# Modulation sums in pairs, table work ordered behind a weight product, one scan for both directions, first norms' squares on TensorE

## The chip, the cores and the metric

The kernel runs on one core of a Trainium2 chip. The metric is the device time of one execution in microseconds. Three timed runs of the kernel before took 3287.81, 3289.54 and 3294.22 us; the median is 3289.54. One further execution was taken with the hardware profiler, and all durations below are from that one.

## What is computed

One layer of a diffusion backbone on 256 latent tokens (`x`) and 256 context tokens (`ctx`), width 2048, everything in float32. Cut to the parts that the change touches:

```python
mod   = silu(c) @ w_ada + b_ada          # 18432 columns: shift, scale, gate of 3 sublayers
mod_c = silu(c_ctx) @ w_ada + b_ada      # the same weights for the context

def ffn(x, m, gain, wg, wu, wd):         # sublayers 1 and 3
    h = rmsnorm(x, gain) * (1 + m.scale) + m.shift
    return x + 0.5 * m.gate * ((silu(h @ wg) * (h @ wu)) @ wd)

x, ctx = ffn(x, mod[0], ...), ffn(ctx, mod_c[0], ...)
proj   = modulated_norm(x, mod[1]) @ w_in           # [S5 | hyena v,x1,x2 | gate_A | gate_B]
proj_c = modulated_norm(ctx, mod_c[1]) @ w_in[:, :1024]
for direction in (forward, reverse):                # 64 groups x 64 complex states
    last  = scan(proj_c)                            # s[t] = Abar * s[t-1] + Bbar u[t]
    y    += Re(C @ scan(proj[S5], start=last))
mixed = (sigmoid(gate_A) * glu(y) + sigmoid(gate_B) * hyena(proj)) @ w_out
x = x + mod[1].gate * mixed
x = ffn(x, mod[2], ...)
return rmsnorm(x, final_g)
```

Each weight is read once per execution.

## The kernel before

**Products.** A float32 weight piece is loaded, cast on ACT to a high part (`wh`, L177, 128x2048) and its rest is made by two DVE subtractions (`wl`, L181, 128x1024 each). Activations are split likewise. `mm3` (L184 to L187) adds three 128x512 matmuls of the type fp32r into one PSUM bank: high by high, high by low, low by high; `mmc` (L194, L196) does it with the activations' two parts side by side.

**Order.** The order in which each engine runs its instructions is fixed when the program is built: a scheduler runs a timeline of its own and places each instruction when that timeline says its inputs are there. `tc.issue_after(ins)`, which the change uses, adds one more condition: the instruction stands behind `ins` on its engine.

**Stages** (us of the profiled execution). From 0 to about 136: the first modulation columns on PE (`ada_pe`, L218 to L238, bank `adacc`, then transposes by a selection matrix, `adsum` L233), the S5 constants, the hyena filters (`kps`, `aps`, `sps`, `hps`), and the first norms (`rstd_of`): 16 squares on ACT per stream, added on DVE (latent, `xl`) and POOL (context, `xc`) at L315. From 136 to 1745: the first FFN, 22 column blocks of 6 weight pieces (gate `pg`, up `pu`, down `pd`), 132 steps of 48 matmuls. At each step `background()` advances two generators: two steps of `ada_rest`, one of `s5_tables`.

`ada_rest` makes the other modulation columns: DVE multiplies raw columns of `w_ada` by the vector and sums them into an accumulator `ac` (L253, L255, 128x512); a matmul with a 128x32 matrix of ones adds the 128 partitions into 32 rows of a bank (L260), ACT copies the 32 rows (L261), and four transposes close a group of four. `ada_vec` does 6 groups of two column blocks with two vectors each (`ns` is 2: latent and context) and 4 groups of four blocks with one (`ns` is 1): 40 sums in all.

`s5_tables` makes, for 8 blocks q and 2 directions d, products on POOL (`win`, cmul at L597 and L600), their transposes on PE (`wtp`, L889, two sets of four), products on POOL (`gt`, L901 and L904) and kernel taps on PE (`kp`, L914, two sets of eight 32-column matmuls in four row groups). `adacc`, its transposes, `wtp` and `kp` all use the one bank of the pool `pc`.

From 1745 on: the up and S5 projections, context carries (a tree of complex products, DVE for direction 0 and POOL for direction 1, L1067 to L1075), then the latent scan, about 1963 to 2034: 31 steps of five `tensor_tensor`, direction 0 on DVE and direction 1 on POOL (L1085 to L1089), with the read-out `yb` (L1111) behind it. PE's work beside it is the output gates, 16 calls of `project` (one is 96 matmuls of 128x256, with the same casts and subtractions for its weights). Then the hyena branch, the merge, the second FFN, to 3283.

Of the kernel before, what the change touches and what calls it, by code (L numbers as in the profile page):

```python
# [19 lines left out]
P = 128  # L20
# [108 lines left out]
def _body(tc, nc, I, out, dbg, es):  # L129
# [53 lines left out]

    def mm3(ps, H, L, xH, xL, first, last):  # L184
# [53 lines left out]
    def ada_vec(nts, ap_):  # L238


        ns = 2 if nts[0] < 20 else 1
        sb = ap_.tile([P, 512], F32, name="adsb", tag="adsb", bufs=1)
        per = 4 // ns
        for i, nt in enumerate(nts):
            acc = [ap_.tile([P, 512], F32, name=f"ac{s}", tag=f"ac{s}", bufs=1) for s in range(ns)]
            for q in range(8):
                raw = ap_.tile([P, 2, 512], F32, name="raw2", tag="raw2", bufs=2)
                sync.dma_start(raw, w_ada[q * 256:(q + 1) * 256, nt * 512:(nt + 1) * 512].rearrange("(k p) n -> p k n", p=P))
                for g in range(2):
                    k = q * 2 + g  # L250
                    for s in range(ns):
                        if k == 0:
                            dve.tensor_scalar(acc[s], raw[:, g], S32[:, k, s:s + 1], None, op0=ALU.mult)  # L253
                        else:
                            dve.scalar_tensor_tensor(acc[s], raw[:, g], S32[:, k, s:s + 1], acc[s], op0=ALU.mult, op1=ALU.add)  # L255
# [47 lines left out]
    def rstd_of(tp, streams, sq, pl, tg):  # L303
# [3 lines left out]
        ns = len(streams)  # L307
        for k in range(KD):
            for xs, r, eng in streams:
                if k == 0:  # L310
# [45 lines left out]
    def prescale(T, sub, xs, s):  # L356


        for i in range(4):
            sh = modT[:, sub * 3 * KD + 4 * i:sub * 3 * KD + 4 * i + 4, s:s + 1].to_broadcast([P, 4, 2])  # L360
            act.copy(T[i][:, :, 516:518], sh)
            dve.tensor_tensor(T[i][:, :, 0:2], sh, T[i][:, :, 516:518].bitcast(F32), ALU.subtract)
            dve.tensor_copy(T[i][:, :, 258:260], zero.unsqueeze(2).to_broadcast([P, 4, 2]))
        for k, t in enumerate(pieces(T)):
            g = gsc[sub][:, k, s:s + 1]
            h, l = both(t)[:, 1], both(t)[:, 0]
            act.activation(h, xs[k], AF.Identity, scale=g)
            dve.scalar_tensor_tensor(l, xs[k], g, h.bitcast(F32), op0=ALU.mult, op1=ALU.subtract)
# [415 lines left out]
    def ada_first():  # L784
# [4 lines left out]
        rstd_of(py, ((xl, r1[0], dve),), ("sq", 2), pb, "b")  # L789
# [4 lines left out]
        rstd_of(py, ((xc, r1[1], pool),), ("sq", 2), pb, "b")  # L794
# [59 lines left out]
    def s5_tables(tp):  # L854

        kv = kD.rearrange("(b r) q (g n) -> r b (q g) n", b=4, g=2)
        for q in range(8):
# [14 lines left out]
            for d in range(2):  # L872
# [33 lines left out]
                yield  # L906
                for g2 in range(2):
                    kp = pc.tile([P, P], F32, name="kp", tag="c")
                    hs = slice(64 * g2, 64 * g2 + 64)
                    for ri in range(2):  # L910
                        for b4 in range(4):
                            e0 = d
                            bo = ((d * 2 + ri) * 4 + b4) * 16
                            pe.matmul(kp[32 * b4:32 * b4 + 32, :], bc_[hs, bo:bo + 32],  # L914
                                      gt[hs, b4, ri, e0:e0 + 8, :].rearrange("p e h -> p (e h)"), start=(ri == 0), stop=(ri == 1))
# [89 lines left out]
    prescale(hT, 1, xl, 0)  # L1005
    prescale(cT, 1, xc, 1)
# [29 lines left out]

    lamp_cm, lamp = open_pool("scan")
    Vl = lamp.tile([P, 2, 2, 32, 33], F32, name="Vl")
# [39 lines left out]
    sd_cm, sdp = open_pool("s5out", side="right")  # L1078
    for k in range(31):
        for d, eng in ((0, dve), (1, pool)):  # L1080
            cur = Vl[:, d, :, :, (32 - k if d else k)]
            nxt = Vl[:, d, :, :, (31 - k if d else k + 1)]
            m1 = sdp.tile([P, 2, 32], F32, name="q1", tag=f"q1{d}", bufs=2)
            m2 = sdp.tile([P, 2, 32], F32, name="q2", tag=f"q2{d}", bufs=2)
            eng.tensor_tensor(m1, cur, LR8[:, 0, d], ALU.mult)  # L1085
            eng.tensor_tensor(m2, cur, LI8[:, 0, d], ALU.mult)
            eng.tensor_tensor(m1, m1, nxt, ALU.add)
            eng.tensor_tensor(nxt[:, 0], m1[:, 0], m2[:, 1], ALU.add)
            eng.tensor_tensor(nxt[:, 1], m1[:, 1], m2[:, 0], ALU.add)  # L1089
# [50 lines left out]

    def project(src, x, kd, tile_of):

        ps = [tile_of() for _ in range(2)]
        for kh in range(kd // 8):
            H, L = wpiece(src[kh * 1024:(kh + 1) * 1024, :].rearrange("(k p) n -> p k n", p=P), 8, 256)
            for k in range(8):
                kk = kh * 8 + k
                for m in range(2):
                    mmc(ps[m], H[:, k, m * P:(m + 1) * P], L[:, k, m * P:(m + 1) * P], x[kk], kk == 0, kk == kd - 1)
        return ps  # L1150

    def bank_a():
        return pa.tile([P, 512], F32, name="prj", tag="a")
    gateD = dp.tile([16, P, 512], F32, name="gateD")
    for g in range(16):
        ps = project(w_in[:, 4096 + g * 256:4096 + (g + 1) * 256], h2, KD, bank_a)
        sg_ = lampg.tile([P, 2, SEQ], F32, name="sgo", tag="sgo", bufs=2)
        for m in range(2):
            total(sg_[:, m], ps[m])
        act.activation(sg_, sg_, AF.Sigmoid)  # L1160
        sync.dma_start(gateD[g], sg_.rearrange("p a n -> p (a n)"))
# [135 lines left out]
    prescale(p3, 2, xl, 0)  # L1297
# [44 lines left out]
```

## Time and profile before

| | before |
|---|---|
| median of 3 runs | 3289.54 us (3287.81 to 3294.22) |
| the profiled execution's own time | 3284.65 us |
| its span in the trace | 3282.9 us |
| PE (matmul) busy | 3154.6 us, 96% |
| PE weight load busy | 2551.6 us, 78% |
| DVE busy | 2374.2 us, 72% |
| ACT busy | 1117.4 us, 34% |
| POOL busy | 636.6 us, 19% |
| HBM read | 588.61 MB, mean 191 GB/s read and written |

A matmul's recorded end is modelled and overlaps its follower; the distance from one start to the next is what it occupies. In the rows, a matmul on full float32 data is recorded more than once: a 128x512 sum by `ones` counts x2, a 64x128 `kp` counts x2.

### The profile page before, as it was taken

How to read it: one execution, taken by the hardware profiler on the slowest of the kernel's cores; microseconds unless marked ns; L12 is line 12 of the kernel's file. 1: busy time of each engine (PE TensorE's matmuls, PEld its weight loads, DVE VectorE, ACT ScalarE, POOL GpSimd, SP SyncE). 2: the span in 40 equal slices, each digit the busy share in tenths (PEclk: the TensorE clock that was granted, in tenths of full speed). 3: DMA queues.
4: the chain of work that ended last, by engine and by line, in shares of the span. 5: the costliest groups of instructions: out<-in, count | busy, mean ns of one | idle time of the engine just before them, and what ended most of it. 6: DMA issues, size and time to landing. Idle time of an engine off the chain costs nothing.

```text
span 3282.9 us, 44026 instructions
## 1 busy us (share of the span) xinstructions
PE 3154.6 (96%) x17118; PEld 2551.6 (78%) x17118; DVE 2374.2 (72%) x3855; ACT 1117.4 (34%) x1492; POOL 636.6 (19%) x758
## 2 busy tenths in 40 slices
PE   6999999999999999999999888999999999999997
PEld 2477677777777877778788877888888888888886
DVE  6578797997986667756656477488887666776677
ACT  4323122222222222222225333545555444344344
POOL 2255564565340000000001057012100000000000
PEclk9999999999999999999999999999999999999998
DMA  8776565555567565556533667755665555555553
GB/s 278 255 256 195 181 204 170 180 192 167 189 212 226 195 192 176 183 180 192 179 97 110 152 222 244 256 180 186 198 208 180 180 185 187 180 183 189 192 192 103
DMA packets 479383, 625.98 MB, mean 191 GB/s; under 512 B 39399, under 2 KB 352328, under 8 KB 478920
## 3 DMA queue, kind: packets, MB, share of 16 engines
q1 hardware_dynamic: 479176, 623.17, 59.2%
q8 instruction: 135, 2.21, 0.3%
q14 instruction: 72, 0.59, 0.1%
HBM read 588.61 MB, written 38.70 MB: 191 GB/s over the span
## 4 chain that ended last, share of the span: by engine, by line
PE 78%; DVE 8%; POOL 7%; DMA 3%; issue 2%; ACT 1%; SPq 0%; DVEq 0%; POOLq 0%; ACTq 0%
PE prj L194 9%; PE pg L194 5%; PE pu L194 5%; PE pd L194 5%; PE prj L196 4%; PE pd L185 4%; PE pg L187 4%; PE pg L185 4%; PE pg L186 4%; PE pd L186 4%; PE pd L187 4%; PE pu L185 4%; PE pu L187 4%; PE pu L186 4%; DVE ac L255 2%; PE pu L196 2%
## 5 line engine op out<-in xcount | busy, mean ns | idle before, releaser
L181 DVE TENSOR_TENSOR wl<-raw,wh 128x1024 fp32r<-128x1024 f32 x736 | 907.3, 1272 | 349.7 <-ACT wh L177 344.4
L177 ACT CAST wh<-raw 128x2048 fp32r<-128x2048 f32 x368 | 702.9, 1910 | 975.4 <-PE pd L186 217.3
L255 DVE SCALAR_TENSOR_TENSOR ac<-raw,S,ac 128x512 f32<-128x512 f32 x600 | 499.3, 861 | 130.5 <-DMA raw<-in_w_ada_dram 125.1
L194 PE MATMUL prj<-h,wh 128*128 128x512 f32 x896 | 322.2, 405 | 0.0
L185 PE MATMUL pd<-ah,wh 128*128 128x512 f32 x704 | 281.1, 400 | 15.6 <-DVE xc L944 8.8
L187 PE MATMUL pu<-h1H,wl 128*128 128x512 f32 x704 | 276.1, 396 | 3.1 <-DVE wl L181 3.1
L186 PE MATMUL pd<-al,wh 128*128 128x512 f32 x704 | 278.4, 396 | 0.0
L185 PE MATMUL pu<-h1H,wh 128*128 128x512 f32 x704 | 278.3, 396 | 0.0
L186 PE MATMUL pu<-h1L,wh 128*128 128x512 f32 x704 | 278.0, 395 | 0.0
L186 PE MATMUL pg<-h1L,wh 128*128 128x512 f32 x704 | 276.8, 393 | 0.0
L187 PE MATMUL pd<-ah,wl 128*128 128x512 f32 x704 | 276.1, 395 | 0.0
L185 PE MATMUL pg<-h1H,wh 128*128 128x512 f32 x704 | 276.0, 394 | 0.0
L187 PE MATMUL pg<-h1H,wl 128*128 128x512 f32 x704 | 274.8, 394 | 0.4 <-DVE wl L181 0.4
L196 PE MATMUL prj<-h,wl 128*128 128x256 f32 x840 | 237.0, 289 | 11.3 <-DVE wl L181 11.3
L194 PE MATMUL pd<-ahl,wh 128*128 128x512 f32 x704 | 242.0, 397 | 2.4 <-DVE xl L513 1.7
L194 PE MATMUL pg<-h,wh 128*128 128x512 f32 x672 | 240.3, 398 | 3.4 <-DVE nt L488 3.4
L194 PE MATMUL pu<-h,wh 128*128 128x512 f32 x672 | 241.3, 396 | 0.0
L194 PEld LDWEIGHTS prj<-h,wh 128*128 128x128 f32 x896 | 169.2, 193 | 36.5 <-DVE h L344 0.7
L1321 POOL TENSOR_TENSOR ft<-ft,nr 128x1024 f32<-128x1024 f32 x1 | 2.8, 2844 | 917.8 <-ACT nr L334 917.8
L944 DVE SCALAR_TENSOR_TENSOR xl<-pd,gate,xl 128x256 f32<-128x256 f32 x314 | 150.6, 480 | 41.4 <-PE pd L187 41.1
L185 PEld LDWEIGHTS pd<-ah,wh 128*128 128x128 f32 x704 | 133.1, 189 | 57.5 <-issue 21.1
L196 PE MATMUL pu<-h,wl 128*128 128x256 f32 x630 | 177.3, 281 | 0.0
(459 smaller groups left out, 6061.5 us busy)
## 6 DMA issues: line engine op xcount, KB each, us to landing
raw<-in_w_ada_dram SPq DMA_DIRECT2D x224, 512.0 KB, 4.4
raw<-in_ffn_w_gate_dram SPq DMA_DIRECT2D x88, 1024.0 KB, 5.1
raw<-in_ffn_w_up_dram SPq DMA_DIRECT2D x88, 1024.0 KB, 5.1
raw<-in_ffn_w_down_dram SPq DMA_DIRECT2D x88, 1024.0 KB, 5.5
raw<-in_w_in_dram SPq DMA_DIRECT2D x64, 1024.0 KB, 6.0
raw<-in_w_ada_dram SPq DMA_DIRECT2D x32, 1024.0 KB, 6.9
raw<-in_w_pa_dram SPq DMA_DIRECT2D x16, 1024.0 KB, 5.4
raw<-in_w_out_dram SPq DMA_DIRECT2D x16, 1024.0 KB, 5.3
```

What stands on the lines that cost most here:

```text
L177: act.copy(H, raw)
L181: dve.tensor_tensor(L[:, hs], raw[:, hs], H[:, hs].bitcast(F32), ALU.subtract)
L185: pe.matmul(ps, H, xH, start=first, stop=False)
L186: pe.matmul(ps, H, xL, start=False, stop=False)
L187: pe.matmul(ps, L, xH, start=False, stop=last)
L194: pe.matmul(ps.rearrange("p (a n) -> p a n", a=2), H, x, start=first, stop=last)
L196: pe.matmul(ps[:, SEQ:], L, x[:, 1], start=False, stop=False)
L255: dve.scalar_tensor_tensor(acc[s], raw[:, g], S32[:, k, s:s + 1], acc[s], op0=ALU.mult, op1=ALU.add)
L944: dve.scalar_tensor_tensor(x, p_, gate[0][:, dc, s:s + 1], x, op0=ALU.mult, op1=ALU.add)
L1321: eng.tensor_tensor(t, t, r4.unsqueeze(1).to_broadcast([P, k1 - k0, SEQ]), ALU.mult)
```

## The change

Five edits.

1. `ada_vec` holds its sums until there are two of them. The two matmuls with ones then go to neighbouring groups of 32 rows, the first ordered behind the second, and one ACT copy takes 64 rows. With one vector the accumulators alternate between `ac0` and `ac1`.
2. In `s5_tables` the transposes and the tap matmuls get `issue_after(newest[0])`: the last matmul that `mm3` has written out so far. A further `yield` stands between the POOL products and the PE work that reads them, so that a pair (q, d) takes six steps instead of four (72 steps become 104 of 132).
3. The latent scan does both directions in one DVE operation. `Vl` is a flat tile; `at(k)` is a view of it in which direction 0 advances and direction 1 retreats. POOL does no scan. `gates(0)` is written ahead of the context carries; the other 15 calls stay behind the scan.
4. The first norms' squares (`eng` is None) are added by matmuls with ones into four groups of 32 rows of a bank, four per group, and copied out by ACT with a factor 1/32.
5. `prescale` takes the latent and the context stream by turns instead of one after the other.

```diff
     def mm3(ps, H, L, xH, xL, first, last):
...
-        pe.matmul(ps, L, xH, start=False, stop=last)
+        mm = pe.matmul(ps, L, xH, start=False, stop=last)
+        newest[0] = getattr(mm, "ins", mm)
...
+        acc = []
         for i, nt in enumerate(nts):
-            acc = [ap_.tile([P, 512], F32, name=f"ac{s}", tag=f"ac{s}", bufs=1) for s in range(ns)]
+            new = [ap_.tile([P, 512], F32, name="ac", tag=f"ac{(i + s) % 2 if ns == 1 else s}", bufs=1) for s in range(ns)]
...
+            acc += new
+            if len(acc) < 2:
+                continue
+
             ps = pc.tile([P, 512], F32, name="adacc", tag="c")
-            for s in range(ns):
-                r0 = 32 * (i * ns + s)
-                pe.matmul(ps[r0:r0 + 32, :], ones32, acc[s], start=True, stop=True)
-                act.copy(sb[r0:r0 + 32, :], ps[r0:r0 + 32, :])
+            r0 = 32 * (i * ns + ns - 2)
+            mm = pe.matmul(ps[r0 + 32:r0 + 64, :], ones32, acc[1], start=True, stop=True)
+            with tc.issue_after(getattr(mm, "ins", mm)):
+                pe.matmul(ps[r0:r0 + 32, :], ones32, acc[0], start=True, stop=True)
+            act.copy(sb[r0:r0 + 64, :], ps[r0:r0 + 64, :])
+            acc = []
...
+        for xs, r, eng in streams:
+            if eng is None:
+                ps = pl.tile([P, 512], F32, name="ssq4", tag=tg)
+                for k in range(KD):
+                    q = tp.tile([P, SEQ], F32, name="sq", tag=sq[0], bufs=sq[1])
+                    act.activation(q, xs[k], AF.Square)
+                    g = k % 4
+                    pe.matmul(ps[32 * g:32 * g + 32, :SEQ], ones32, q, start=(k < 4), stop=(k >= KD - 4))
+                act.activation(r, ps[:, :SEQ], AF.Identity, scale=1.0 / 32.0)
...
-        rstd_of(py, ((xl, r1[0], dve),), ("sq", 2), pb, "b")
+        rstd_of(py, ((xl, r1[0], None),), ("sq", 2), pb, "b")
...
                 yield
+                yield
                 wt = tp.tile([P, 4, 2, P], F32, name="wt", tag="wg", bufs=2)
                 for bh in range(2):
                     ps = pc.tile([P, 4, P], F32, name="wtp", tag="c")
-                    for x4 in range(4):
-                        pe.transpose(ps[:, x4, :], win[:, bh * 2 + x4 // 2, x4 % 2].rearrange("p j h -> p (j h)"), ident)
+                    with tc.issue_after(newest[0]):
+                        for x4 in range(4):
+                            pe.transpose(ps[:, x4, :], win[:, bh * 2 + x4 // 2, x4 % 2].rearrange("p j h -> p (j h)"), ident)
...
+    gates(0)
...
+    def at(k):
+
+        n = 2144 - 2 * k
+        return Vf[:, k:k + 2 * n].rearrange("p (d n) -> p d n", d=2)[:, :, 0:2080:33]
...
     for k in range(31):
-        for d, eng in ((0, dve), (1, pool)):
...
+        cur, nxt = at(k), at(k + 1)
+        m1 = sdp.tile([P, 2, 64], F32, name="q1", tag="q1", bufs=2)
+        m2 = sdp.tile([P, 2, 64], F32, name="q2", tag="q2", bufs=2)
+        tt(m1, cur, LRf, ALU.mult)
+        tt(m2, cur, LIf, ALU.mult)
+        tt(m1, m1, nxt, ALU.add)
+        tt(nxt[:, :, :32], m1[:, :, :32], m2[:, :, 32:], ALU.add)
+        tt(nxt[:, :, 32:], m1[:, :, 32:], m2[:, :, :32], ALU.add)
```

(The `kp` matmuls get the extra `yield` and the condition just as the transposes do, and the context's `rstd_of` the same None.)

How the built programs differ at three places. First PE in the first FFN, a modulation sum among the products of `pu` (h1H and h1L are the high and low weights' counterparts of the normed input); before:

```order
L187 MATMUL pu<-h1H_1019,wl 128x512
L185 MATMUL pu<-h1H_1019,wh 128x512
L186 MATMUL pu<-h1L_1020,wh 128x512
L260 MATMUL adacc<-ac_1522,ones_77 32x512
L187 MATMUL pu<-h1H_1019,wl 128x512
L185 MATMUL pu<-h1H_1021,wh 128x512
L186 MATMUL pu<-h1L_1022,wh 128x512
```

and after, where the sums are L267 and L269:

```order
L188 MATMUL pu<-h1L_1024,wh 128x512
L189 MATMUL pu<-h1H_1023,wl 128x512
L187 MATMUL pu<-h1H_1023,wh 128x512
L267 MATMUL adacc<-ac,ones_77 32x512
L269 MATMUL adacc<-ac,ones_77 32x512
L188 MATMUL pu<-h1L_1024,wh 128x512
L189 MATMUL pu<-h1H_1023,wl 128x512
L187 MATMUL pu<-h1H_1025,wh 128x512
```

A sum stood alone, its partner some 23 rows later; now two stand in a row. Over the stage, 40 single sums become 17 such pairs and 6 sums that still stand alone.

Second, PE in the same stage at a set of taps (`kp`, eight matmuls in all); before, the later six of a set whose first two stand 20 rows earlier:

```order
L185 MATMUL pu<-h1H_1017,wh 128x512
L914 MATMUL kp<-gt,bc__3626 32x128 x4
L186 MATMUL pu<-h1L_1018,wh 128x512
L187 MATMUL pu<-h1H_1017,wl 128x512
L185 MATMUL pu<-h1H_1019,wh 128x512
L186 MATMUL pu<-h1L_1020,wh 128x512
L187 MATMUL pu<-h1H_1019,wl 128x512
L914 MATMUL kp<-gt,bc__3626 32x128 x2
L185 MATMUL pu<-h1H_1019,wh 128x512
L186 MATMUL pu<-h1L_1020,wh 128x512
L187 MATMUL pu<-h1H_1019,wl 128x512
```

and after:

```order
L187 MATMUL pu<-h1H_1043,wh 128x512
L188 MATMUL pu<-h1L_1044,wh 128x512
L941 MATMUL kp<-gt,bc__3468 32x128 x8
L189 MATMUL pu<-h1H_1043,wl 128x512
L187 MATMUL pu<-h1H_1043,wh 128x512
L188 MATMUL pu<-h1L_1044,wh 128x512
L189 MATMUL pu<-h1H_1043,wl 128x512
```

The set came in up to three pieces; now its eight stand together. Over the stage `kp` stands in 51 places before (22 times all eight, 29 times fewer) and in 34 after (31 times all eight); `wtp` in 38 places before and 35 after; all insertions together in 139 and in 103.

Third, DVE at the beginning of the latent scan (`q` are its products, `wl` the weights of a gate); before, one direction, while POOL has a row like these for the other:

```order
L1085 TENSOR_TENSOR q_14512<-Vl,LRI_14026 128x64
L1086 TENSOR_TENSOR q_14513<-Vl,LRI_14026 128x64
L1087 TENSOR_TENSOR q_14512<-q_14512,Vl 128x64
L1088 TENSOR_TENSOR Vl<-q_14512,q_14513 128x32
L1089 TENSOR_TENSOR Vl<-q_14512,q_14513 128x32
L1085 TENSOR_TENSOR q_14526<-Vl,LRI_14026 128x64
L1086 TENSOR_TENSOR q_14527<-Vl,LRI_14026 128x64
L181 TENSOR_TENSOR wl<-raw,wh 128x1024 x2
L1087 TENSOR_TENSOR q_14526<-q_14526,Vl 128x64
L1088 TENSOR_TENSOR Vl<-q_14526,q_14527 128x32
L1089 TENSOR_TENSOR Vl<-q_14526,q_14527 128x32
```

and after, both directions (L606 is the helper `tt`):

```order
L606 TENSOR_TENSOR q_14580<-Vl,LRI_14094 128x128
L606 TENSOR_TENSOR q_14581<-Vl,LRI_14094 128x128
L606 TENSOR_TENSOR q_14580<-q_14580,Vl 128x128
L606 TENSOR_TENSOR Vl<-q_14580,q_14581 128x2x32 x2
L181 TENSOR_TENSOR wl<-raw,wh 128x1024 x2
L606 TENSOR_TENSOR q_14587<-Vl,LRI_14094 128x128
L606 TENSOR_TENSOR q_14588<-Vl,LRI_14094 128x128
L606 TENSOR_TENSOR q_14587<-q_14587,Vl 128x128
L606 TENSOR_TENSOR Vl<-q_14587,q_14588 128x2x32 x2
```

Five operations of half the elements on each of two engines become five on one; the subtractions for the gate's weights stand between them as before.

## Rows read from the trace of the kernel before

**Rows 1.** The page's first part: engine, busy us (share), instructions.

```profile
PE 3154.6 (96%) x17118; PEld 2551.6 (78%) x17118; DVE 2374.2 (72%) x3855; ACT 1117.4 (34%) x1492; POOL 636.6 (19%) x758
```

**Rows 2.** Busy us by window: us, PE, PEld, DVE, ACT, POOL, clock, DMA, GB/s.

```profile
176.00:1000.00 824.00, 791.41 (x3766) 601.65 (x3765) 687.65 (x955) 199.45 (x237) 431.78 (x480) 0.99 0.61 193
476.00:488.00 12.00, 8.82 (x30) 6.50 (x29) 10.73 (x11) 2.90 (x3) 11.53 (x15) 0.72 0.52 153
550.00:600.00 50.00, 50.00 (x241) 37.73 (x240) 49.74 (x76) 11.28 (x14) 27.07 (x36) 1.00 0.63 203
1963.00:2034.00 71.00, 62.87 (x361) 51.88 (x359) 68.56 (x188) 27.84 (x27) 66.31 (x151) 0.98 0.72 229
```

**Rows 3.** PE timeline (start us, us, ...) around one modulation sum.

```profile
1283.62 0.39 PE L185 MATMUL pg<-h1H,wh 128*128 128x512 f32 x1
...
1284.08 0.39 PE L187 MATMUL pg<-h1H,wl 128*128 128x512 f32 x1
1284.40 1.04 PE L260 MATMUL adacc<-ac,ones 128*32 128x512 f32 x2
...
1285.72 0.40 PE L186 MATMUL pu<-h1L,wh 128*128 128x512 f32 x1
```

**Rows 4.** PE timeline around four such matmuls in four row groups.

```profile
168.66 0.40 PE L187 MATMUL pu<-h1H,wl 128*128 128x512 f32 x1
168.99 1.06 PE L225 MATMUL adacc<-raw,S 128*32 128x512 f32 x8
...
170.33 0.39 PE L186 MATMUL pu<-h1L,wh 128*128 128x512 f32 x1
```

**Rows 5.** PE timeline around eight `kp` matmuls at once.

```profile
286.61 0.40 PE L187 MATMUL pg<-h1H,wl 128*128 128x512 f32 x1
286.94 0.64 PE L914 MATMUL kp<-gt,bc__1538 64*32 64x128 f32 x16
...
287.85 0.40 PE L186 MATMUL pg<-h1L,wh 128*128 128x512 f32 x1
```

**Rows 6.** PE timeline around a piece of two `kp` matmuls.

```profile
270.03 0.40 PE L187 MATMUL pd<-ah,wl 128*128 128x512 f32 x1
270.36 0.41 PE L914 MATMUL kp<-gt,bc__1538 64*32 64x128 f32 x4
...
271.04 0.40 PE L186 MATMUL pd<-al,wh 128*128 128x512 f32 x1
```

**Rows 7.** PE's waits, 176 to 1745: waiting for, us in total, times, longest.

```profile
PE kp L914 <- POOL gt L904: 5.6, 5, 2.1
PE wtp L889 <- POOL win L597: 5.4, 3, 3.2
PE wtp L889 <- POOL win L600: 4.6, 5, 1.7
```

**Rows 8.** PE timeline in the first stage: four sums and transposes by turns.

```profile
115.57 1.04 PE L225 MATMUL adacc<-raw,S 128*32 128x512 f32 x2
...
120.72 0.69 PE L740 MATMUL kps<-hwo,hr 64*128 64x512 f32 x1
```

**Rows 9.** PE's longest wait for DVE in 0 to 176.

```profile
PE adacc L225 <- DVE adsb L230: 5.2, 1, 5.2
```

**Rows 10.** DVE's sums by form, 300 to 900 and 1000 to 1600: busy, mean ns.

```profile
L255 DVE SCALAR_TENSOR_TENSOR ac<-raw,S,ac 128x512 f32<-128x512 f32 x288 | 250.6, 918 | 33.9 <-DMA raw<-in_w_ada_dram 32.7
...
L255 DVE SCALAR_TENSOR_TENSOR ac<-raw,S,ac 128x512 f32<-128x512 f32 x192 | 144.1, 750 | 73.5 <-DMA raw<-in_w_ada_dram 70.5
```

**Rows 11.** DVE timeline: one scan step from start to start.

```profile
1982.07 0.27 DVE L1085 TENSOR_TENSOR q<-Vl,LRI 128x64 f32<-128x64 f32 x1
...
1983.15 0.28 DVE L1085 TENSOR_TENSOR q<-Vl,LRI 128x64 f32<-128x64 f32 x1
```

**Rows 12.** DVE by form, 1895 to 2045: subtractions and products: busy us, mean ns.

```profile
L181 DVE TENSOR_TENSOR wl<-raw,wh 128x1024 fp32r<-128x1024 f32 x40 | 53.1, 1360 | 15.1 <-ACT wh L177 11.4 <-issue 3.7
...
L1068 DVE TENSOR_TENSOR m<-tr,LRI 128x256 f32<-128x256 f32 x2 | 1.9, 958 | 0.0
```

More of the change, by code (lines that the diff above doesn't have):

```diff
@@ L354, in both, with prescale @@
         return t[:, 2:].rearrange("p (a n) -> p a n", a=2)[:, :, :SEQ] if t.shape[-1] == WX else t.rearrange("p (a n) -> p a n", a=2)
-    def prescale(T, sub, xs, s):
+    def prescale(sub, streams):
         for i in range(4):
[L360 to L368, printed above, removed]
+            for T, xs, s in streams:
+                sh = modT[:, sub * 3 * KD + 4 * i:sub * 3 * KD + 4 * i + 4, s:s + 1].to_broadcast([P, 4, 2])
+                act.copy(T[i][:, :, 516:518], sh)
+                dve.tensor_tensor(T[i][:, :, 0:2], sh, T[i][:, :, 516:518].bitcast(F32), ALU.subtract)
+                dve.tensor_copy(T[i][:, :, 258:260], zero.unsqueeze(2).to_broadcast([P, 4, 2]))
+        for k in range(KD):
+            for T, xs, s in streams:
+                g = gsc[sub][:, k, s:s + 1]
+                t = both(pieces(T)[k])
+                act.activation(t[:, 1], xs[k], AF.Identity, scale=g)
+                dve.scalar_tensor_tensor(t[:, 0], xs[k], g, t[:, 1].bitcast(F32), op0=ALU.mult, op1=ALU.subtract)
     def mmp(ps, H, L, x, first, last):
@@ L906, in s5_tables @@
                 yield
+                yield
                 for g2 in range(2):
@@ L909, in s5_tables @@
                     hs = slice(64 * g2, 64 * g2 + 64)
[L910 to L915, printed above, removed]
+                    with tc.issue_after(newest[0]):
+                        for ri in range(2):
+                            for b4 in range(4):
+                                e0 = d
+                                bo = ((d * 2 + ri) * 4 + b4) * 16
+                                pe.matmul(kp[32 * b4:32 * b4 + 32, :], bc_[hs, bo:bo + 32],
+                                          gt[hs, b4, ri, e0:e0 + 8, :].rearrange("p e h -> p (e h)"), start=(ri == 0), stop=(ri == 1))
                     if d == 0:
@@ L1004, in _body @@
     cT = [n2p.tile([P, 4, WX], FR, name=f"hc{i}") for i in range(4)]
-    prescale(hT, 1, xl, 0)
-    prescale(cT, 1, xc, 1)
+    prescale(1, ((hT, xl, 0), (cT, xc, 1)))
     rstd_of(n2p, ((xl, r2[0], dve), (xc, r2[1], pool)), ("sq", 4), pc, "c")
@@ L1034, in _body, with project, bank_a, gates @@
     close(xcp_cm)
+    def project(src, x, kd, tile_of):
+        ps = [tile_of() for _ in range(2)]
+        for kh in range(kd // 8):
+            H, L = wpiece(src[kh * 1024:(kh + 1) * 1024, :].rearrange("(k p) n -> p k n", p=P), 8, 256)
+            for k in range(8):
+                kk = kh * 8 + k
+                for m in range(2):
+                    mmc(ps[m], H[:, k, m * P:(m + 1) * P], L[:, k, m * P:(m + 1) * P], x[kk], kk == 0, kk == kd - 1)
+        return ps
+    def bank_a():
+        return pa.tile([P, 512], F32, name="prj", tag="a")
+    gateD = dp.tile([16, P, 512], F32, name="gateD")
+    def gates(g):
+        ps = project(w_in[:, 4096 + g * 256:4096 + (g + 1) * 256], h2, KD, bank_a)
+        sg_ = lampg.tile([P, 2, SEQ], F32, name="sgo", tag="sgo", bufs=2)
+        for m in range(2):
+            total(sg_[:, m], ps[m])
+        act.activation(sg_, sg_, AF.Sigmoid)
+        sync.dma_start(gateD[g], sg_.rearrange("p a n -> p (a n)"))
+    gates(0)
     lamp_cm, lamp = open_pool("scan")
-    Vl = lamp.tile([P, 2, 2, 32, 33], F32, name="Vl")
+    Vf = lamp.tile([P, 4288], F32, name="Vl")
+    Vl = Vf[:, :4224].rearrange("p (d r g c) -> p d r g c", d=2, r=2, g=32)
     LRI = lamp.tile([P, 2, 5, 2, 2, 32], F32, name="LRI2")
@@ L1078, in _body @@
     sd_cm, sdp = open_pool("s5out", side="right")
+    def at(k):
+        n = 2144 - 2 * k
+        return Vf[:, k:k + 2 * n].rearrange("p (d n) -> p d n", d=2)[:, :, 0:2080:33]
+    LRf, LIf = (t[:, 0].rearrange("p d r g -> p d (r g)") for t in (LR8, LI8))
     for k in range(31):
-        for d, eng in ((0, dve), (1, pool)):
[L1081 to L1089, printed above, removed]
+        cur, nxt = at(k), at(k + 1)
[6 more added lines that the diff above has]
+        tt(nxt[:, :, 32:], m1[:, :, 32:], m2[:, :, :32], ALU.add)
     ysb = sdp.tile([P, 8, 16, 16], F32, name="ysb")
@@ L1138, in _body @@
     close(sd_cm)
[L1141 to L1161, printed above, removed]
+    for g in range(1, 16):
+        gates(g)
     ybx = [mpp.tile([P, 2, SEQ], FR, name=f"ybx{k}") for k in range(8)]
@@ L1296, in _body @@
     p3 = [b3p.tile([P, 4, WX], FR, name=f"p3{i}") for i in range(4)]
-    prescale(p3, 2, xl, 0)
+    prescale(2, ((p3, xl, 0),))
     banks3 = []
```

9 lines of the change are left out of this document (6 added, 3 removed).

## The prediction

> **What bounds the kernel now.** I read the page's busy times first: PE is busy in 96% of the span, DVE in 72%, ACT in a third, POOL in a fifth [rows 1]. So a microsecond counts only where PE runs something it need not run, waits, or runs at a lower clock. The windows come next. In the first FFN up to 1000, PE is busy 791.41 of 824 us, and DVE is close behind with 687.65; in 550 to 600 DVE is busy 49.74 of 50 [rows 2]. That is the part to keep in mind: a faster PE meets DVE there. Then the PE timeline, where the distance from one start to the next is what a matmul occupies. Two 128x512 products lie 0.46 us apart in 1283.62 to 1284.08 [rows 3], so one takes 0.23. Where something is inserted among the products, its price is the distance across it less 0.46 for the two products in that distance. Last the waits of PE: in the whole stage those for POOL's tables sum to 15.6 us [rows 7].
>
> **The change part by part.**
>
> *Sums in pairs.* Across one modulation sum: 1285.72 - 1284.08 = 1.64, less 0.46 is 1.18 us [rows 3]. There are 40, so 47.2 us. What two in neighbouring row groups cost, the trace doesn't show; it shows one (1.18) and four at once: 170.33 - 168.66 = 1.67, less 0.46 is 1.21 [rows 4]. Four cost what one costs, so two lie between, and I take 1.2. After the change 17 pairs and 6 singles stand in PE's order, 23 insertions by 1.2 or 27.6. Saved: 19.6. If the second of a pair ran behind the first (1.18 + 1.18), the 17 pairs would save nothing; that end is a rival below. The 20 ACT copies that go lie on an engine that is idle two thirds of the span: nothing.
>
> *Taps and transposes behind a product.* A `kp` set of eight costs 287.85 - 286.61 - 0.46 = 0.78 [rows 5]; a piece of two costs 271.04 - 270.03 - 0.46 = 0.55 [rows 6]. So it is the interruption that costs, not the number. Before: 22 x 0.78 + 29 x 0.55 = 33.1; after: 31 x 0.78 + 3 x 0.55 = 25.8. Saved: 7.3. The transposes stand in 38 places before and 35 after; I count them at nothing (3 places by 0.55 are 1.7 at most).
>
> *The extra yield.* PE waits for POOL 13 times: 5.6 + 5.4 + 4.6 = 15.6 us [rows 7]. They come up where POOL is late by up to 3.2 us with a product that PE has in order next. With the extra step of 48 matmuls by 0.23, or 11 us, between product and reader, a lateness of 3.2 is covered, so I expect all 15.6 to go. What is late next: POOL's next products wait for a free `wg` slot and are started a step later too, and a pair (q, d) now has six steps, 66 us, for what POOL did in four (POOL was busy 431.78 of 824, 52% [rows 2]); 72 steps become 104 of 132, so there is room. The instructions queued behind such a wait are the FFN products themselves, which is why a short wait costs its full length. The table's stores on SP move with their step and nobody reads them before 1745.
>
> *The clock after a wait.* In 476 to 488, the window of the 3.2 us wait, the granted clock is 0.72 [rows 2]: PE ran at the lower of its two levels (1.2 instead of 2.4 GHz) for part of 12 us after it had stood still. 12 x 0.28 = 3.4 us of full-speed time are lost there, and part of that is the wait itself. A wait of 2.1 [rows 7] may do the same on a smaller scale. I take 3.4 for all; bounds 0 and 7.
>
> *DVE takes some back.* The four terms sum to 19.6 + 7.3 + 15.6 + 3.4 = 45.9. Some four fifths of it falls before 1000 or so, where DVE is busy 83%, and in stretches like 550 to 600 wholly. There PE can't get ahead of the subtractions that make `wl`. DVE's operations are slowed where POOL works: one `ac` sum takes 918 ns in 300 to 900, beside POOL, and 750 in 1000 to 1600, almost without it [rows 10]. The change spreads the same POOL work over 104 steps instead of 72, so per step a third less of that slowing falls. I deduct 5 us; bounds 0 and 20. The Trainium skill's page "SBUF — State Buffer" (section "SBUF: two separate sides") says that DVE and GpSimd share a pair of ports as an exclusive lock, held for a whole instruction while the loser is blocked. By that rule spreading moves DVE's blocked time but removes none of it; the deduction would then be nearer to the rival "DVE is the second bound" than to 5. The trace agrees that beside POOL the same operation is longer (918 against 750 ns), but doesn't tell whether it was fully blocked.
>
> *First norms.* 15 DVE additions per latent stream and 15 on POOL go; 32 matmuls of 128x256 by ones come, in chunks of one to eight on PE. In row groups several cost what one costs [rows 4], and here half the columns: some 17 chunks by 0.6 at most, about 10 us, of which part fills waits. On the other side: PE waits 5.2 us for a DVE copy that stands behind such additions [rows 9], and in PE's order three of the four places where four sums and four transposes alternate become two blocks. Such a place takes 120.72 - 115.57 = 5.15 us [rows 8]; in blocks, 1.2 for the sums and at most 1.3 for the transposes (0.32 each, (5.15 - 4 x 0.97) / 4): 2.6 saved by each, 8 by three. Sum: 10 - 5.2 - 8, or -3; I take -4 and bounds -12 and +8, because this stage also waits for loads.
>
> *The scan.* Before, DVE is busy 68.56 of 71 us, POOL 66.31, PE 62.87 [rows 2]: three engines nearly full, PE with gates as filler. A step of five operations takes 1.08 us on DVE [rows 11]. Doubling the elements (three operations by 64 more, two by 32 more) I price by the distance between an operation of 64 elements (1.08 / 5 = 0.216) and one of 512 (0.750 [rows 10]): 0.0012 per element, so 3 x 0.076 + 2 x 0.038 = 0.30. That gives 1.38 by 31, or 43 us. Between them stand 24 subtractions for the gates' weights by 1.36 at most [rows 12], 32.6. Sum 75.6, beside the 71 of now; the 1.36 holds POOL's influence, which is gone. PE has one more gate call (96 products) ahead of the read-out, so a scan that is 5 us longer doesn't show. I take 0, bounds -5 and +5; the upper end of the operation's price is a rival.
>
> *`prescale` by turns, the first gate's place:* both engines run the same instructions in nearly the same order; 0.
>
> **Sum.** -45.9 + 5 - 4 + 0 = -44.9 against the profiled execution's own 3284.65: 3239.8. That execution lay 4.9 below the median of the three runs (3289.54), so I expect a median of **3244** to be compared with 3289.54, rounded down by a microsecond for transposes: 3243.
>
> **Rivals.**
> *DVE is the second bound (B).* For: 49.74 of 50 busy [rows 2], and an `ac` sum that is 22% longer beside POOL [rows 10]. Against: on average over 176 to 1000 DVE has 136 us left, more than the gain. If a third of that window (275 us) can't become faster, a third of what was to be won there is lost, some 13 us, with the 5 already in the sum: 3243 + 13 - 3 = 3253; if two thirds, 3266.
> *The edits don't do what they say (C).* Two sums in neighbouring row groups run one after the other (19.6 lost), and POOL is late by a whole step, so that the waits and the clock's fall stay (19.0 lost), and the first stage stays as it is (4): 3243 + 43 = 3286, no change. Against: four in a row show 1.21 [rows 4].
> *The scan becomes the path (D), slower.* A two-input operation of 128x256 in the carries takes 0.958 us, beside POOL [rows 12]. If the view that runs in two directions makes each of the 155 operations cost that, DVE needs 155 x 0.958 + 32.6 = 181 us where 71 were; PE has one more gate call (96 x 0.115, half of 0.23 for half the columns: 11 us) to fill it: +99, or 3342. PE begins to wait from (71 + 11 - 32.6) / 155 = 0.32 us per operation, and the kernel is slower than before from about 0.61. Against: the operations of the scan have the same stride of 33 elements as before and take 0.216 a piece.
>
> **How the numbers follow.** My forecast 62%, B 25%, C 6%, D 5%, something that gains more 2%. The range: below, all terms whole and both stages at their good ends: 3243 - 5 - 8 - 5 - 4 = 3221; I put 3218 for the clock's upper bound. Above, B with two thirds and a little of the first stage's bad end: 3268. About 0.2% (6.6 us) is what a measurement of this kernel tells from no change; faster holds the forecast, B, the small rest and a little of C: 0.90; the same 0.05, slower 0.05.
>
> **What would show it.** Across a pair in the PE timeline 1.2, not 2.4, less the products. No PE wait for `win` or `gt` of more than a microsecond, and a clock of 1.00 throughout 176 to 1000. POOL's table work reaching to about 1300. The first FFN product earlier than the 136 of now by a few us. The stage of the scan about as long as 71 us, with the operations near 0.28 us. I am wrong if DVE is the releaser of PE's waits for `wl` in 176 to 1300 by more than 10 us in all (B), or if the read-out waits for the scan (D).

## The result and the profile after

The changed kernel takes 3249.76 us (median of 4 runs, 3249.12 to 3251.05), the kernel before on the same chip 3290.26 (4 runs): ratio 0.9876, 95% interval 0.9859 to 0.9893, 40.5 us less. The forecast was 3243, range 3218 to 3268. The profiled execution took 3250.28 us with a span of 3248.5; against the one of before (3284.65, span 3282.9) that is 34.4 us, and the rest of the 40.5 is that the profiled execution of before lay 5.6 below its median and that of after 0.5 above.

The page's first part after, to be read against [rows 1]:

```profile
PE 3134.8 (97%) x17182; PEld 2556.9 (79%) x17182; DVE 2336.7 (72%) x3840; ACT 1104.8 (34%) x1474; POOL 533.4 (16%) x588
```

To find the place of the 34.4 us I cut both spans at the same pieces of work in the PE timeline: first FFN product, first up projection, first `vps`, first `ztp` of the hyena branch, first product of the second FFN, last matmul.

| stage (us) | before | after | difference | forecast |
|---|---|---|---|---|
| start, to the first FFN product | 135.7 | 126.2 | -9.5 | -4 |
| first FFN | 1618.0 | 1598.3 | -19.7 | -40.9 |
| up and S5 projections | 96.2 | 96.2 | 0.0 | 0 |
| carries, scan, read-out | 288.0 | 282.0 | -6.0 | 0 |
| hyena, to the second FFN | 370.5 | 370.4 | -0.1 | 0 |
| second FFN, final norm to its last matmul | 762.8 | 763.8 | +1.0 | 0 |

The total is near the forecast, its parts are not: half of the gain expected of the first FFN is missing, and the start and the scan gave 11.5 us more than forecast. These are single executions. In four profiled kernels that do nothing new in the first FFN (before and the two scan and one norm runs below) that stage took 1618.0 to 1623.1 us, and the one of before is the shortest of them.

The windows of after (columns as in [rows 2]; the third is the scan's 71 us, which now begin at 1933):

```profile
176.00:1000.00 824.00, 795.64 (x3711) 622.87 (x3710) 659.56 (x972) 191.06 (x208) 314.07 (x360) 0.98 0.59 189
550.00:600.00 50.00, 50.00 (x245) 38.51 (x244) 40.08 (x65) 11.62 (x10) 14.36 (x23) 1.00 0.61 195
1933.00:2004.00 71.00, 70.69 (x409) 60.31 (x408) 69.56 (x182) 30.43 (x31) 2.28 (x6) 1.00 0.76 244
```

In 176 to 1000 PE is busy only 4 us more of 824 than before, and the granted clock is 0.98, not the 1.00 that I named as the sign of success. In the scan's window PE went from 62.87 busy to 70.69 and POOL from 66.31 to 2.28.

**The insertions.** PE timeline across a pair in the first FFN, and the records of each of its two sums:

```profile
551.52 0.39 PE L189 MATMUL pd<-ah,wl 128*128 128x512 f32 x1
551.84 0.62 PE L267 MATMUL adacc<-ac,ones 128*32 128x512 f32 x1
551.85 0.62 PE L269 MATMUL adacc<-ac,ones 128*32 128x512 f32 x1
552.29 0.59 PE L267 MATMUL adacc<-ac,ones 128*32 128x512 f32 x1
552.30 0.59 PE L269 MATMUL adacc<-ac,ones 128*32 128x512 f32 x1
...
553.16 0.40 PE L188 MATMUL pd<-al,wh 128*128 128x512 f32 x1
```

The two sums start 0.01 us apart. Across them 553.16 - 551.52 - 0.46 = 1.18 us, exactly what one alone cost [rows 3]. Summed over the stage, by the distances across each insertion without waiting time, sums by ones went from 47.1 us to 28.4, taps from 34.4 to 25.7 and table transposes from 17.6 to 16.6: 28.4 us less.

**The waits.** PE's waits in the first FFN (columns as in [rows 7]); the largest before beside those of [rows 7]:

```profile
PE pd L185 <- DVE xc L944: 8.8, 3, 4.1
...
PE pd L185 <- ACT sil L442: 4.2, 1, 4.2
PE pu L187 <- DVE wl L181: 3.1, 2, 1.8
```

and the six largest after:

```profile
PE pd L187 <- ACT sil L465: 10.4, 4, 3.8
PE pu L189 <- DVE wl L181: 7.5, 3, 4.0
PE wtp L914 <- POOL win L623: 4.9, 4, 2.1
PE pd L187 <- DVE xc L971: 4.4, 4, 3.0
PE adacc L267 <- DVE ac L259: 4.4, 1, 4.4
...
PE pg L189 <- DVE wl L181: 2.2, 3, 1.0
```

No wait for `gt` is left, and of those for `win` 6.3 us of 10.0. But the waits for ACT and DVE have grown. By engine, between the first FFN product and the first up projection, with the products that ran at the lower clock (their distance to the next is 0.40 to 0.46 us instead of 0.23, so each loses 0.2):

| | POOL | DVE | ACT | all waits | products at the lower clock |
|---|---|---|---|---|---|
| before | 15.8 | 15.5 | 4.2 | 36.6 | 30 |
| after | 6.3 | 20.7 | 11.7 | 38.7 | 49 |

(1.1 us of the first line wait for a load.) So against the 9.5 us of waits for POOL that went stand 12.7 us more for DVE and ACT. One of them in full, all engines but PE in a stretch of after (start us, duration, engine, [idle before and its releaser]), and PE's wait:

```profile
914.39 3.37 DVE L181 TENSOR_TENSOR wl<-raw,wh 128x1024 fp32r<-128x1024 f32 x2
915.14 1.54 POOL L924 TENSOR_TENSOR ta<-bc__6812,pq__6810 128x288 f32<-128x288 f32 x1
916.65 1.65 POOL L925 TENSOR_TENSOR tb<-bc__6812,pq__6810 128x288 f32<-128x288 f32 x1
917.69 1.16 DVE L468 TENSOR_TENSOR al<-sil,ah 128x512 fp32r<-128x512 f32 x1
918.38 1.12 POOL L926 TENSOR_TENSOR gt<-ta,tb 128x288 f32<-128x288 f32 x1
918.77 1.27 DVE L259 SCALAR_TENSOR_TENSOR ac<-raw,S,ac 128x512 f32<-128x512 f32 x1
918.88 0.60 ACT L465 ACTIVATE sil<-pg 128x512 f32<-128x512 f32 x1 [5.54 <-DVE al L468]
919.53 0.50 PE L187 MATMUL pd<-ah,wh 128*128 128x512 f32 x1 [2.06 <-ACT sil L465]
```

Read from below: PE's next `pd` needs a bank that ACT frees by reading `pg` into `sil`; `sil` has one buffer, which is free only after DVE's `al`; `al` stands behind two `wl`, and these take 3.37 us while POOL is busy throughout. The same pair takes 2.35 us at 1943.52, where POOL is idle.

### The profile page after: what moved, and what is told of

Read it like the earlier page. It is cut to its first block, busy times and chain, and to the rows that moved or that the text cites. A ratio compares the mean times of both kernels' runs of the same rounds, so it can differ in the third digit from the quotient of the medians.

```text
span 3248.5 us, 43933 instructions
## 1 busy us (share of the span) xinstructions
PE 3134.8 (97%) x17182; PEld 2556.9 (79%) x17182; DVE 2336.7 (72%) x3840; ACT 1104.8 (34%) x1474; POOL 533.4 (16%) x588
## 4 chain that ended last, share of the span: by engine, by line
PE 79%; DVE 10%; DMA 6%; issue 2%; ACT 2%; POOL 1%; SPq 0%; DVEq 0%; POOLq 0%; ACTq 0%
PE prj L197 8%; PE pu L197 5%; PE pg L197 5%; PE pd L197 5%; PE pg L189 4%; PE pu L189 4%; PE pu L187 4%; PE pg L188 4%; PE pg L187 4%; PE pd L187 4%; PE pu L188 4%; PE pd L188 4%; PE pd L189 4%; PE prj L199 4%; DMA raw<-in_w_ada_dram 3%; DVE wl L181 3%
## 5 line engine op out<-in xcount | busy, mean ns | idle before, releaser
L259 DVE SCALAR_TENSOR_TENSOR ac<-raw,S,ac 128x512 f32<-128x512 f32 x600 | 474.1, 820 | 143.6 <-DMA raw<-in_w_ada_dram 138.4
L187 PE MATMUL pd<-ah,wh 128*128 128x512 f32 x704 | 280.8, 400 | 16.1 <-ACT sil L465 10.4
L187 PEld LDWEIGHTS pd<-ah,wh 128*128 128x128 f32 x704 | 133.5, 190 | 55.1 <-ACT sil L465 13.3
L199 PEld LDWEIGHTS prj<-h,wl 128*128 128x128 f32 x840 | 162.4, 194 | 15.7 <-DVE wl L181 10.7
```

What stands on the lines that cost most here:

```text
L199: pe.matmul(ps[:, SEQ:], L, x[:, 1], start=False, stop=False)
L259: dve.scalar_tensor_tensor(new[s], raw[:, g], S32[:, k, s:s + 1], new[s], op0=ALU.mult, op1=ALU.add)
```

## The experiments

Each ran beside the kernel before on the same chip. The kernel before had medians of 3289.4 to 3293.8 us there, so ratios are what is compared. Stage lengths are from each kernel's profiled execution, cut as above; single executions differ by some us in a stage that an edit doesn't touch.

**Each part alone.**

*Sums in pairs.*

```diff
-            for s in range(ns):
-                r0 = 32 * (i * ns + s)
-                pe.matmul(ps[r0:r0 + 32, :], ones32, acc[s], start=True, stop=True)
+            mm = pe.matmul(ps[r0 + 32:r0 + 64, :], ones32, acc[1], start=True, stop=True)
+            with tc.issue_after(getattr(mm, "ins", mm)):
+                pe.matmul(ps[r0:r0 + 32, :], ones32, acc[0], start=True, stop=True)
```

> The kernel before with the sums in pairs and nothing else. Theory A (the edits' prices stand alone, something else ate a part in the whole): 40 insertions of 1.18 us become about 23 of 1.2 to 1.25, so -18 to -20 us against before. Theory B (DVE is the second bound of the first FFN, so whatever is taken from PE comes back as waits for DVE): -5 to -12 us, and the PE waits for wl and sil in 126 to 1750, 8 us in the kernel before, grow to 12 or more. In both the distance across a pair less two products is 1.2 to 1.3.

Measured: ratio 0.9970 (0.9954 to 0.9987), about 10 us. PE's waits grew from 36.6 to 50.7 us: POOL 15.8 to 24.3, ACT 4.2 to 9.3. Some 20 us less of insertions and 14 more of waits, and over 50 products at the lower clock: theory B's number, but not its engine alone, since most of what came back was POOL. The first FFN took 1615.4 us, only some 3 to 8 less than where nothing is changed in it. So half or more of what the pairs save is already lost here, with POOL's work spread as before. POOL's busy time in the stage is the same (436 us, 440 before); that its products are late the more against a quicker PE is the likely reason, not shown by itself.

*Table work.*

```diff
                 yield
+                yield
...
+                    with tc.issue_after(newest[0]):
```

> The kernel before with the table work ordered behind the newest product and the extra yields, and nothing else. Theory A: -20 to -26 us (7 for taps in one piece, 15.6 for the waits on POOL, 3 for the clock). Theory B: -5 to -15 us, with the waits on POOL near 6 instead of 15.6 (as in the changed kernel) and the waits for wl, sil and xc grown by 10 us or more.

Measured: ratio 0.9935 (0.9921 to 0.9950), 21 us, theory A's size; the first FFN 1604.1. Waits for POOL 3.7 us, for DVE and ACT 25.4 instead of 19.7, among them one that was 0.6 before:

```profile
PE adacc L263 <- DVE ac L258: 12.2, 4, 5.9
```

These are single sums that PE has in order before DVE's chain for them has ended. Alone, the part keeps most of its gain.

*Scan.*

```diff
-        for d, eng in ((0, dve), (1, pool)):
+        cur, nxt = at(k), at(k + 1)
+        tt(m1, cur, LRf, ALU.mult)
```

> The kernel before with the scan of both directions on DVE and the first gate ahead of the carries. In the changed kernel the stretch from the first vps to the first ztp is 6.1 us shorter (282.0 against 288.1). If that is the scan's own doing: -5 to -7 us here. If it came from the other edits' shifts (the order of the later stages): within 2 us of before.

Measured: ratio 0.9972 (0.9960 to 0.9984), the stretch 281.7 us against 288.0. The scan, or the first gate's place that this edit moves with it, does it; a run below separates the two.

*First norms.*

```diff
-        rstd_of(py, ((xl, r1[0], dve),), ("sq", 2), pb, "b")
+        rstd_of(py, ((xl, r1[0], None),), ("sq", 2), pb, "b")
```

> The kernel before with the first norms' squares added on TensorE and nothing else. In the changed kernel the first FFN product starts at 126.2 instead of 135.7 us. If the norms do that: -8 to -10 us here. If part of it comes from the other edits, or if the first FFN loses it again to loads, -2 to -6 us.

Measured: ratio 0.9962 (0.9949 to 0.9974), first FFN product at 125.2 us. The norms do it. The four reductions sum to 1.61%, and the whole change brings 1.24%. Each is known to about 0.14, but all four are measured against the same runs of the kernel before, so the sum is known to about 0.4 only (estimated by drawing from the single runs), and whether the parts add up can't be told. (Edit 5 was not run alone.)

**The scan without the gate's place.**

```diff
-    gates(0)
...
-    for g in range(1, 16):
+    for g in range(16):
```

> The kernel before with the scan of both directions in one DVE operation, but all sixteen gates left behind the scan in the program. With the first gate ahead the ratio to before was 0.9972 and the stretch from the first vps to the first ztp 281.7 us against 288.0. If the scan itself saves that: stretch 281 to 284, ratio 0.996 to 0.998. If the first gate's place does: stretch 286 to 290, ratio 0.999 to 1.001.

Measured: ratio 0.9980 (0.9970 to 0.9991), the stretch 284.4 us (from the first `vps` at 1855.28), the one ahead of it 97.5 instead of 96.2. The ratio agrees with the scan itself, and the stretch lies just above its 284. Over all profiled kernels the stretch took 288.0 to 292.1 us in the six with the old scan and 280.7 to 285.4 in the eight with the new one, so the scan does it. What the gate's place gives, 2.7 us between these two executions, can't be told from that scatter.

**Order without the extra step.**

```diff
-                yield
                 yield
                 wt = tp.tile([P, 4, 2, P], F32, name="wt", tag="wg", bufs=2)
```

(from the table work alone, at both places)

> The kernel before with the table's transposes and taps ordered behind the newest product but without the extra yields. Both yields and order together gave a ratio of 0.9935. If the extra step is what takes the waits on POOL away: here the pieces merge (7 us) but PE waits for win and gt stay at 15 us or grow, ratio 0.997 to 1.000. If the order alone does it (the taps stand later than the products they interrupt): ratio 0.993 to 0.995, with the waits on POOL under 5.

Measured: ratio 1.0001 (0.9992 to 1.0011), waits for POOL 18.1 us, `kp` still in pieces of two and four. So `issue_after` alone brings nothing, not even the merging that the expectation granted it; the extra step that lets POOL finish first is needed. Whether the step would do without the condition was not run.

**Half of the sums left out, in both kernels.**

```diff
-                for g in range(2):
+                for g in range(1):
                     k = q * 2 + g
```

> The changed kernel with half of the accumulating DVE operations of the modulation sums left out (300 instead of 600; loads, matmuls and everything else stay; the modulation columns so made are not the reference's). Together with the same cut in the kernel before it asks what the change is worth when DVE has room. Theory B (DVE is the second bound of the first FFN): PE's waits for wl, sil, xc and ac in 126 to 1750, 30 us in the changed kernel, fall to under 10, the first FFN falls from 1598 to about 1575, and it is 30 us or more shorter than the kernel before with the same cut. Theory A (the edits themselves cost more than their prices, by the order they force): the first FFN stays above 1590, and the difference to the kernel before with the same cut stays near 20.

> The kernel before with the same half of the accumulating DVE operations left out (columns not the reference's). Theory B: PE's waits for POOL stay (10 to 16 us), since they are not DVE's doing, the waits for DVE go, and the first FFN falls from 1618 by 5 to 12 us only. Theory A: it falls as much as the changed kernel does.

Measured: ratios 0.9805 (0.9791 to 0.9818) for the changed kernel and 0.9941 (0.9929 to 0.9953) for the one before; first FFN 1573.9 and 1596.5 us, 22.6 apart where the full kernels are 19.7 apart. Waits in all: 25.6 (from 38.7) and 21.0 (from 36.6). (Neither kernel makes the reference's columns.) The 1573.9 is what theory B named (about 1575; theory A 1590 or more); the rest went against it: 22.6 where it expected 30 or more, and waits for DVE and ACT of 24.8 us in the changed kernel where it expected under 10. DVE's work does cost PE time, but half of its sums cost PE about as much in the kernel before (21.5 us of the first FFN) as in the changed one (24.4), so they don't explain why the change fell short.

**The modulation work spread evenly.**

```diff
+            due += 1.65 if at_ < 118 else 2.3
+            m = max(int(due) - at_, 1)
+            at_ += m
-            n = sum(next(ada, 0) is None for _ in range(2))
+            n = sum(next(ada, 0) is None for _ in range(m))
```

> The changed kernel with the modulation work spread evenly: 1.65 instead of 2 advances a step while each advance holds four DVE sums (two vectors), 2.3 where it holds two; nothing is left out. Theory B: DVE's load falls from about 7 to 6 us a step before 700 and rises after 1000, where it has room; PE's waits for DVE and ACT in 126 to 1750 fall from 30 to 15 or less, and the kernel is 8 to 15 us faster than the changed kernel (about 3278 less 38 on this chip's scale, a ratio to before of 0.983 to 0.985). If the waits are only a matter of single misplaced instructions: within 4 us of the changed kernel, ratio 0.987 to 0.989.

Measured: 3241.90 us, ratio 0.9850 (0.9837 to 0.9863); the first FFN 1587.2, 11 us less than the changed kernel's. This is the fastest kernel of the study that computes everything, by 0.26% (the two weren't run side by side, and their intervals touch). The time came as theory B said, the waits didn't: 34.9 in all instead of under 15, so 3.8 us are waits and 1.4 the clock (42 products at the lower one instead of 49). Another 4.9 us lie in insertions, by the distances across them (21 places with sums instead of 23, and fewer for `wtp` and `kp`); about 1 us is left. So nearly half of this gain is another order on PE and not fewer waits.

**`al` ahead of `wl`.** The wait shown above suggests that order.

```diff
+                if m == 0:
+                    held[0] = getattr(sub, "ins", sub)
...
+            if held[0] is not None:
+                with tc.issue_after(held[0]):
+                    dve.tensor_tensor(L[:, hs], raw[:, hs], H[:, hs].bitcast(F32), ALU.subtract)
```

> The changed kernel with one more condition: the next weight piece's first subtraction (wl) on DVE stands behind the first subtraction of the hidden activations (al). In the changed kernel PE waits 10.4 us in 4 places for ACT's sil: its one buffer is held until al is done, and al stands on DVE behind two wl subtractions. Theory C (the waits come from this place in DVE's order): the waits for sil fall under 4 us, PE's idle time in 125 to 1760 falls from 42 to about 34, and the ratio to before is 0.984 to 0.986 (the changed kernel: 0.9876). Rival (DVE simply has too much to do, so another operation is late instead): the waits for wl or xc grow by what sil loses, idle stays near 42, ratio 0.987 to 0.989.

> The evenly spread modulation work (ratio to before 0.985) together with the condition on wl and al. Theory C: waits for sil from 12.2 to under 4, ratio 0.981 to 0.983. Rival: ratio 0.984 to 0.986.

Measured: ratios 1.0049 (1.0034 to 1.0065) and 1.0033 (1.0022 to 1.0044), slower than before, as neither theory said. PE's largest waits in the first of the two:

```profile
PE pd L193 <- ACT sil L471: 25.0, 17, 4.0
PE pd L193 <- DVE sil L472: 15.5, 6, 6.5
```

and a wait of DVE's own, 0.5 us in the changed kernel:

```profile
DVE al L474 <- ACT ah L473: 20.1, 14, 2.5
```

The first FFN went to 1658.1 us and PE's waits to 75.8. `al` needs ACT's cast `ah`, so a `wl` behind it has to wait for ACT too, and with it the rest of DVE's row. As a remedy theory C is out. Whether the waits of the changed kernel come from this place in DVE's order the runs don't tell, since the edit brought waits of its own.

**POOL's products taken away.**

```diff
-                    cmul(pool, win[:, h, 0], win[:, h, 1], wpw(0)[:, h], wpw(1)[:, h], rv(raw_(0, d, 0), 8)[:, h],
-                         rv(raw_(0, d, 1), 8)[:, h], ta[:, :, 0:8], tb[:, :, 0:8])
+                    for ri in range(2):
+                        act.copy(win[:, h, ri], rv(raw_(0, d, ri), 8)[:, h])
```

(and so for `gt`; the preparation of `br` and `bi` left out)

> The changed kernel without the table's products on POOL: ACT copies of operands of the same shapes stand in their place (32 pairs of copies for win, 32 for gt), so that the tables, and with them the output, are not the reference's; transposes, taps, stores, sums and order conditions stay. Theory P (POOL's work makes DVE's operations longer, and the waits for DVE and ACT follow POOL through the stage): the ac sums take 0.75 us on average instead of 0.82, a pair of wl about 2.35 instead of up to 3.4, PE's waits for DVE and ACT in 126 to 1735 fall from 35 to under 15, those for POOL from 6 to 0, and the first FFN falls from 1598 to 1570 to 1578 us; ratio to before 0.979 to 0.982. Rival (the order on DVE, with its single sil buffer, makes the waits, whoever works beside it): waits for DVE and ACT stay above 25, the first FFN is 1588 or more, ratio 0.984 to 0.987.

Measured: ratio 0.9754 (0.9741 to 0.9768), more than theory P expected, and not the rival's. First FFN 1557.8 us, 40.5 less than the changed kernel's; waits for DVE 9.0 and ACT 4.3, for POOL none, 13.3 in all; 7 products at the lower clock. That makes 25.4 us of waits and 8.4 of the clock (42 products by 0.2); some 4 more are fewer insertions. DVE's sums and subtractions in the page of after, and in that of this kernel:

```profile
L181 DVE TENSOR_TENSOR wl<-raw,wh 128x1024 fp32r<-128x1024 f32 x736 | 900.3, 1263 | 365.2 <-ACT wh L177 363.9
...
L259 DVE SCALAR_TENSOR_TENSOR ac<-raw,S,ac 128x512 f32<-128x512 f32 x600 | 474.1, 820 | 143.6 <-DMA raw<-in_w_ada_dram 138.4
```

```profile
L181 DVE TENSOR_TENSOR wl<-raw,wh 128x1024 fp32r<-128x1024 f32 x736 | 880.3, 1236 | 371.4 <-ACT wh L177 369.9
...
L259 DVE SCALAR_TENSOR_TENSOR ac<-raw,S,ac 128x512 f32<-128x512 f32 x600 | 429.0, 746 | 166.1 <-DMA raw<-in_w_ada_dram 161.5
```

The same 600 sums are 45 us shorter. Beside POOL single operations are stretched by half and more (3.37 for a `wl` pair instead of 2.35, 1.27 for a sum instead of 0.75). That these are the ones that PE waits for shows only in part: of its six waits for `wl` after, four end on a subtraction of 1.21 or 1.22 us, which is its time alone, and two on one of 1.64 and 1.67. In the longest (4.01 us, at 360) the stretched operations stand further up in DVE's row, behind a wait for a load:

```profile
351.49 4.20 DVE L259 SCALAR_TENSOR_TENSOR ac<-raw,S,ac 128x512 f32<-128x512 f32 x4 [1.61 <-DMA raw<-in_w_ada_dram]
...
358.93 2.35 DVE L181 TENSOR_TENSOR wl<-raw,wh 128x1024 fp32r<-128x1024 f32 x2
```

The four sums took 4.20 us where four alone take 3.0.

## Why the prediction held in sum and not in its parts

That 3249.76 lies near 3243 is in part luck: the first FFN fell short by 21.2 us, and the start and the scan, for reasons that the sum had at nothing or too small, made up for 11.5 of them. (The forecast's own arithmetic gives 3239.8 + 4.9 = 3244.7 where it goes on with 3244, and for rival B it takes off 3 where the 5 of the sum would be due; neither matters here.)

- **Pairs and taps: right.** A pair costs what a single sum cost (1.18), and the insertions lost 28.4 us where 19.6 + 7.3 were forecast, without a term for the transposes (1.0).
- **The waits: the step that failed.** "A lateness of 3.2 is covered, so I expect all 15.6 to go", plus 3.4 for the clock, less 5 that "DVE takes some back". That is -14. Measured: waits +2.1 and clock +3.8 (19 more products by 0.2), together +5.9. The 28.4 less 5.9 are 22.5 where 19.7 were measured; 2.8 us remain open, less than the 5 by which this stage varies where nothing is changed in it. Three waits for `win` were above the microsecond named as the limit (1.4 to 2.1). Why the waits for DVE and ACT grew is argued and not shown. The deduction's own mechanism, POOL's slowing of DVE, is a candidate: POOL's whole table work costs the changed kernel 40 us, its own lateness included, and the change makes its products no fewer; what it costs the kernel before wasn't run. Before, the last wait of the stage for DVE or ACT other than at its end is at 919 us, with POOL done by 980; after, the last is at 1207, with POOL done by 1300. But with the pairs alone PE still waited for ACT at 1037 (2.4 us) with POOL done by 960, and without POOL's products for DVE at 1159 (2.5 us), so POOL isn't all of it. That PE itself is quicker is the other candidate; the pairs alone, with 14 us more of waits, speak for it.
- **The shared ports.** The deduction named the Trainium skill's rule ("SBUF — State Buffer", section "SBUF: two separate sides"): on the ports they share, DVE and GpSimd exclude each other for whole instructions. From it I had drawn that spreading removes no blocked time. That inference came nearer to the result than my 5. On DVE's own time it went too far: a sum's mean fell from 861 ns in the kernel before to 832 with the table work alone and 820 with the whole change, and 746 are left without POOL, so spreading removed about a quarter of the stretching. Whether an operation is wholly blocked no run shows.
- **Rival B: neither right nor wrong as told.** Its time was 3253, and the result lies between it and the forecast, nearer to B. Its sign, more than 10 us of waits for `wl` in 176 to 1300, was just missed with 9.7. Its reason, that DVE has too little time left, fits the runs only in part: DVE was busy 659.56 of 824 us after, 40.08 of 50 in the stretch that had been full, and halving its sums relieved both kernels alike, by 21.5 and 24.4 us. So DVE's work costs both kernels, and does not explain why the change fell short.
- **First norms: direction right, size off.** -9.5 for -4, and alone -10.5. The wait of 5.2 for DVE's copy [rows 9] shrank to 0.8 as forecast; waits for loads fell too, 16.1 to 12.0, which the sum had held at nothing.
- **Scan: the working was nearly right, the conclusion wrong.** A step takes 1.50 us:

```profile
1939.90 0.70 DVE L606 TENSOR_TENSOR q<-Vl,LRI 128x128 f32<-128x128 f32 x2
...
1941.40 0.72 DVE L606 TENSOR_TENSOR q<-Vl,LRI 128x128 f32<-128x128 f32 x2
```

  for 1.38 forecast, far from the 0.61 an operation at which rival D began. I had written that POOL's influence on `wl` would be gone, and took 0 all the same. It is where the gain is: a `wl` beside the scan took 1.31 us on average before (1963 to 2034) and 1.22 after (1933 to 2004), PE's waits for `wl` in that stage fell from 11.0 to 6.8 us, and those for POOL's end of the scan (2.0) and for `tq` (2.3) went. Before:

```profile
PE prj L196 <- DVE wl L181: 11.0, 9, 3.7
...
PE yb L1111 <- POOL Vl L1088: 2.0, 1, 2.0
```

  and after, all waits of the stage 21.8 us instead of 28.7:

```profile
PE prj L199 <- DVE wl L181: 6.8, 4, 3.7
```

- **Rival C** fell with the pair's 1.18, though its second half, waits and clock that stay, came true in another form.

What stays open: the run without POOL's products took away POOL's lateness and its slowing of DVE at once, and put copies on ACT; how much each is worth, and what the same cut would bring in the kernel before, wasn't run. A second `sil` buffer wasn't tried.

## What to carry to other kernels

When a busy engine is relieved by tens of microseconds, don't credit the removal of its waits: list who feeds it and ask whether they became faster; here 9.5 us of waits for POOL went, 12.7 came for DVE and ACT, and only the removed work counted. A helper engine can cost far more than the waits that carry its name: without POOL's products the stage was 40 us shorter, though PE waited for POOL itself 6.3 us. Matmuls in neighbouring row groups that stand together cost what one does, so collect before you interrupt, and give the producer a step of lead; an order condition without the lead brought nothing.

## What was not expected of the hardware

- Two 128x512 sums in neighbouring row groups started 0.01 us apart and together cost 1.18 us of the stream, as one does.
- DVE operations that run beside POOL's are not slowed evenly: a pair of 128x1024 subtractions took 2.35 us alone and 3.37 where POOL was busy throughout, with two products of 128x288 among its work.
- After the longer waits of PE (4.38 us at 231, 4.01 at 360, 2.46 at 798) products ran at 0.43 us instead of 0.23, the lower of the two clock levels (granted clock 0.54 in the 6 us from 360.2); after 2.06 at 919 they didn't (1.00 in the 6 us from 919.5). There were 49 such products in the first FFN of the changed kernel, about 10 us, and 7 where POOL didn't work.
